# Turning the memory's normalized tokens into channels: squares of 32 on VectorE with a trip through DRAM, in place of identity matmuls

## The chip, the core and the metric

The kernel runs on one core of one Trainium2 chip. A core has TensorE (PE in the profile; its weight loads are listed apart as PEld), VectorE (DVE), ScalarE (ACT), GpSimd (POOL) and SyncE (SP), which here only issues DMAs. Each engine works off its own instructions in order and waits on semaphores for the others. The metric is the device time of one execution in microseconds (us), smaller being better. A change is judged by the medians of several runs before and after.

## What is computed

One layer of a streaming encoder on 512 tokens of 1024 channels. Four mixers run in parallel on the normalized input; their outputs are gated, merged and projected. Then comes cross-attention into 256 memory tokens, then a gated MLP. All inputs are float32. The change touches the way in which the memory tokens reach the cross-attention:

```python
def _rms_norm(x, g):
    y = xf * lax.rsqrt(jnp.mean(xf * xf, axis=-1, keepdims=True) + EPS)
    return (y * g.astype(jnp.float32)).astype(x.dtype)
...
x = x + _rms_norm(mixed, norm_mix_post[l])
hx = _rms_norm(x, norm_x_pre[l])
m = _rms_norm(mem, norm_mem[l])              # mem: (1, 256, 1024)
xq = (hx @ w_xq[l]).reshape(B, S, X_HEADS, X_HEAD_DIM)
xk, xv = jnp.split(m @ w_xkv[l], 2, axis=-1)
```

The product `m @ w_xkv` sums over the 1024 channels. TensorE sums over partitions, so the normalized tokens, which stand with tokens on partitions, must be turned so that channels stand on partitions.

## The kernel before

**Precision.** Every float32 operand of a product is held as two tiles, a rounded high part and the rest. `split` (L152) makes them: ScalarE copies the value into the high tile (L155), VectorE subtracts it from the value and leaves the low tile (L156). A product is three matmuls (`mm3`: high with high, high with low, low with high), all through `matmul` at L232, so L232 carries nearly all of TensorE's work. Weights come in pieces of 512 KB: `load_raw` issues the DMA on SP (L176) into one of two buffers named `wr`; `split_weights` makes `wh` (ScalarE, L190) and `wl` (VectorE, L191), four buffers each. The memory tokens' pair of tiles is `mth` and `mtl`, each 128 partitions x 8 groups of channels x 256 tokens.

**The order of the work.** `run_blocks` (L203) takes jobs one after the other. It traces the load and the split of a job's weights three jobs ahead, then the job's matmuls. Beside the jobs runs a planner, `Background` (L47). It holds generators such as `mem_task`; each `yield cost, wait` says what the step just traced costs and how long, on a clock that adds up the expected time of the matmuls (0.215 us for one over 512 columns), the next step is to be left alone. After each job, and in the middle of a job whose weights have eight groups of channels, `tick` lets due tasks take steps, as far as a credit of 0.7 us for each us of clock allows. `drain` runs a named task to its end. The traced order is not the order in the queues: a scheduler goes through the trace with a timeline of its own, and lays out the instructions of each engine and each DMA queue by when it expects them to be ready. So the queues of SP and ScalarE can stand in another order than the text.

**The stage of the change.** The last of the four mixers' gates is `gate_blocks(1, "f", ...)`: four times two gate jobs (24 matmuls into one PSUM bank, a tanh on ScalarE at L1043) and one branch job (24 matmuls into two banks, VectorE's multiply and add at L1055 and L1056). Banks come from `bank` (L97): here alternately from the names `mm` and `av`, with two banks each; transposes use the name `tr`. `open_last_branch` (L1130) opens the pool `xm`, issues the load of the memory norm's gain on POOL and adds `mem_task` to the planner. When the twelve jobs are traced, `all_jobs` drains `mem`, opens the merge (`open_mix_out`, which takes the tags `s0`, `s1` and `s2` again for two rows of gains and for `m1`), runs its jobs, and only then the first readers of `mth` and `mtl`, `kx_jobs` (L1180).

**The task.** `mem_task` (L1169) works on two blocks of 128 tokens. For each, POOL issues the load of the tokens into `m_t` (tag `s1`, one buffer, L1172), `normed` (L274) squares and sums on ScalarE (L277), makes the factor on POOL (L268, L271) and multiplies on VectorE (L281) into `y_t` (tag `s2`, one buffer, named `mn`). After a wait of 8 `to_channels` (L286) makes eight transposes of 128x128 on TensorE, as matmuls by the identity (L236), four in each of two banks, and splits each bank into `mth` and `mtl`.

**A trip through DRAM that the kernel already makes.** The convolution's output is turned twice, in `conv_norm_task` (L670). VectorE's `transpose` turns every square of 32x32 in place (L676). DMAs on SP write the squares to DRAM at their transposed places (L680), and read them back as rows (L683).

Of the kernel before, what the change touches and what calls it, by code (L numbers as in the profile page):

```python
# [17 lines left out]
F32 = mybir.dt.float32  # L18
# [7 lines left out]
P = 128  # L26
# [3 lines left out]
NK = D // P  # L30
# [53 lines left out]
def hybrid_layer(ctx: ExitStack, tc: tile.TileContext, a: dict, out: bass.AP):  # L84
    nc = tc.nc
    V, A, G, PE, SP = nc.vector, nc.scalar, nc.gpsimd, nc.tensor, nc.sync
# [4 lines left out]
    dram = ctx.enter_context(tc.tile_pool(name="dr", bufs=1, space=DRAM))  # L91
# [5 lines left out]
    def bank(tag=None):  # L97
        if tag is None:
            turn_of.n += 1
            tag = "av" if turn_of.shared and turn_of.n % 2 else "mm"  # L100
        return psum.tile([P, 512], F32, tag=tag, name=f"ps_{tag}", bufs=2)
# [24 lines left out]
    def space(pool, name, n):  # L126

        if n:
            pool.tile([P, n // 4], F32, name=name)

    for i in range(8):
        n = ("wh", "wl")[i % 2]
# [3 lines left out]
        elif i < 6:  # L136
            n = ("fz_raw", "fz", "fe", "fu", "fd")[i - 1]
# [14 lines left out]
    def split(ps, hi, lo, scale=None):  # L152

        if scale is None:
            A.copy(hi, ps)  # L155
            V.tensor_tensor(lo, ps, hi.bitcast(F32), ALU.subtract)  # L156
        else:
            A.activation(hi, ps, AF.Copy if isinstance(scale, float) else AF.Identity, scale=scale)
            V.scalar_tensor_tensor(lo, ps, scale, hi.bitcast(F32), ALU.mult, ALU.subtract)
# [75 lines left out]
    def transpose(ps, x, n=P):  # L235
        PE.transpose(ps, x, ident[:n, :n])  # L236
        bg.clock += 0.107
# [26 lines left out]
    def rstd_of(pool, parts, n=1):  # L264

        m = pool.tile([P, n], F32, tag="st_m", name="st_m", bufs=4)
        r = pool.tile([P, n], F32, tag="st_r", name="st_r", bufs=4)
        G.tensor_tensor(m, parts[0], eps[:, :n], ALU.add)  # L268
        for part in parts[1:]:
            G.tensor_tensor(m, m, part, ALU.add)  # L270
        G.tensor_tensor(r, m, nhalf[:, :n], ALU.pow)  # L271
        return r

    def normed(pool, x_t, gain, y_t, ends=None):  # L274

        ms = pool.tile([P, 1], F32, tag="st_s", name="st_s", bufs=4)
        A.activation(y_t, x_t, AF.Square, scale=1.0 / math.sqrt(D), accum_out=ms)  # L277
        r = rstd_of(pool, [ms])
        n = D // len(gain)
        for i, g in enumerate(gain):  # L280
            end = V.scalar_tensor_tensor(y_t[:, i * n:(i + 1) * n], x_t[:, i * n:(i + 1) * n], r, g, ALU.mult, ALU.mult)  # L281
        if ends is not None:
            ends.append(end.ins)
        return y_t

    def to_channels(y_t, act, t):  # L286

        sl = slice(t * P, (t + 1) * P)
        for half in range(2):
            ps = bank("tr")  # L290
            ks = slice(half * 4, half * 4 + 4)
            for k in range(4):
                transpose(ps[:, k * P:(k + 1) * P], y_t[:, (half * 4 + k) * P:(half * 4 + k + 1) * P])
            split(ps.rearrange("p (k c) -> p k c", k=4), act[0][:, ks, sl], act[1][:, ks, sl])
# [18 lines left out]
    def e4(dtype=F32):  # L313
        return m1p.tile([P, 2, S], dtype, tag="e", name="e", bufs=3)
# [55 lines left out]
    for i, plan in enumerate(plans):  # L370
        r_t = m1p.tile([P, P], F32, tag="fbias" if i == 2 else "ck", name=f"rows{i}", bufs=2)
        n = 0
# [19 lines left out]
    for t in range(2):  # L392
        y_t = m1p.tile([P, D], F32, tag="ptl", name="nt", bufs=2)
# [29 lines left out]
    def turn(t, half):  # L423
        ps = turned[t, half] = bank("av" if half else "tr")
        for k in range(4):
            keep(PE.transpose(ps[:, k * P:(k + 1) * P], y01[t][:, (half * 4 + k) * P:(half * 4 + k + 1) * P], ident))
# [54 lines left out]
    for i in range(2):  # L481
        for p in range(3):
            first_half(i, p, w_g[i], glu[2:])
            if p == 2 - 2 * i:
                with tc.issue_after(casts[-1].ins):
                    y_t = normed(m1p, xs[:, 2 + i], gain, m1p.tile([P, D], F32, tag="ptl", name="nt", bufs=2))
                to_channels(y_t, ht, 2 + i)

    def pc(name, j=0, n=1):
        i, base = where[name]  # L490
        return par[i][:, base + j:base + j + n]
# [89 lines left out]
    def y8(dtype=F32R):  # L581
        return m2p.tile([P, 4, S], dtype, tag="y8", name="y8", bufs=2)
# [73 lines left out]
    def conv_task(j):  # L656
# [5 lines left out]
        for k in range(n - 1):  # L662
# [4 lines left out]
                conv_ends.append(ins.ins)  # L667
            yield 0.66, 0.0

    def conv_norm_task():  # L670
        xn = m1p.tile([P, 5, S], F32, tag="qk", name="xn", bufs=2)
        tok, chan = (dram.tile([S, S], F32, name=n) for n in ("conv_tok", "conv_chan"))

        def turn(rows, squares, src):
            for i in range(4):
                V.transpose(squares[:, i], src[:, i])  # L676
                yield 0.65, 0.0
            form = rows.rearrange("(b r) (j a c) -> a r j b c", r=32, a=4, c=32)
            for a in range(4):
                SP.dma_start(form[a], squares[a * 32:a * 32 + 32].rearrange("r j (b c) -> r j b c", c=32))  # L680
            yield 0.0, 4.0
            for i in range(4):
                SP.dma_start(xn[:, i], rows[i * P:(i + 1) * P, :])  # L683
            yield 0.0, 5.0

        yield 0.0, 2.0
        while len(conv_ends) < 4:
            yield 0.0, 0.5
        yield from turn(tok, conv_u, conv_y)
        for t in range(NT):  # L690
            st = m1p.tile([P, 6], F32, tag="bn6", name="bn6", bufs=2)
            mv = m1p.tile([P, 2], F32, tag="bn2", name="bn2", bufs=2)
            V.bn_stats(st, xn[:, t])
            V.bn_aggr(mv, st)
            r = rstd_of(m1p, [mv[:, 1:2]])
            V.tensor_scalar(xn[:, t], xn[:, t], mv[:, 0:1], r, ALU.subtract, ALU.mult)
            yield 1.5, 0.0
        yield from turn(chan, conv_y, xn)
        while "d" in y:
            yield 0.0, 2.0  # L700
        yield 0.0, 2.0
        y["c"] = (y8(), y8())
        for j in range(4):
            e = e4()
            A.activation(e[:, 0], xn[:, j], AF.Identity, bias=pc("ln_b", j), scale=pc("ln_g", j))
            A.activation(e[:, 1], xn[:, j], AF.Tanh, bias=half["ln_b"][:, j:j + 1], scale=half["ln_g"][:, j:j + 1])
            V.scalar_tensor_tensor(e[:, 0], e[:, 1], 1.0, e[:, 0], ALU.add, ALU.mult)
            split(e[:, 0], y["c"][0][:, j], y["c"][1][:, j], 0.5)
            yield 1.4, 1.0
# [355 lines left out]
    ns = SimpleNamespace()  # L1065
# [8 lines left out]
    def mixer_jobs():  # L1074
        yield from c_jobs()
        yield then(lambda: bg.add(lam_task(), "lam"))
        yield from d_jobs()
        yield then(lambda: bg.add(conv_norm_task(), "conv"))
        wide = m1p.tile([P, NT, D], F32, tag="v", name="wide")
        free = iter([wide[:, i] for i in (0, 1, 2, 3) * 2])  # L1080
# [46 lines left out]
    def stage(tag, name):  # L1127
        return ns.xm.tile([P, D], F32, tag=tag, name=name)

    def open_last_branch():  # L1130
        close(m1)
        close(m2b)
        ns.xm_, ns.xm = new_pool("xm", True)
        ns.mt = (ns.xm.tile([P, NK, MEM], F32R, tag="mth", name="mth"),
                 ns.xm.tile([P, NK, MEM], F32R, tag="mtl", name="mtl"))
        ns.kx = (ns.xm.tile([P, 4, MEM], F32R, name="kxh"), ns.xm.tile([P, 4, MEM], F32R, name="kxl"))
        ns.gain = stage("s0", "g_mem")
        G.dma_start(ns.gain, a["norm_mem"][0].partition_broadcast(P))
        bg.add(mem_task(), "mem")
        ns.mix_, ns.mixp = new_pool("mix", True)  # L1140
        ns.mix, ns.mix_parts, ns.wide = {}, {}, None
        qa = [mix_tile("qa0", 4)]
        hl = [[mix_tile(f"m{i}{q}", 4, F32R) for i in range(2)] for q in range(NK // 2)]
        qa.append(mix_tile("qa1", 4))
        ns.mix_a, ns.mix_b, ns.mix_hl = qa, mix_tile("qb", 12), hl
# [23 lines left out]
    def mem_task():  # L1169
        for t in range(2):  # L1170
            m_t = stage("s1", "m_t")
            G.dma_start(m_t, mem_d[t * P:(t + 1) * P, :])  # L1172
            y_t = normed(ns.xm, m_t, [ns.gain], stage("s2", "mn"))
            if t == 0:
                space(ns.xm, "gap8", 96)
            yield 1.3, 8.0
            to_channels(y_t, ns.mt, t)
            yield 1.2, 0.0

    def kx_jobs():  # L1180
        for h in range(4):
# [573 lines left out]
```

## Time and profile before

| | |
|---|---|
| median of 3 runs | 1061.96 us (1061.37 to 1063.41) |
| the profiled execution | 1061.46 us, of it span of the trace 1059.7 us |
| mean granted clock of TensorE | 0.998 |
| TensorE busy | 1048.7 us |
| VectorE busy | 800.8 us |
| ScalarE busy | 497.9 us |
| moved by DMA | 156.78 MB, mean 148 GB/s |

The span runs from the first to the last instruction of the trace. "Busy" is the time in which an engine had an instruction under way; on TensorE neighbouring matmuls overlap, so that the time from one start to the next is shorter than the duration shown. In lists of instructions a line shows start, duration, engine, line of the program, operation, the tile written and the tiles read, and in brackets the idle time before it with what ended it.

### The profile page before, as it was taken

The numbers are of one execution on the slowest core, as the hardware profiler recorded it, in microseconds if no ns is written. First come the engines' busy times: TensorE is split into PE (matmuls) and PEld (weight loads), VectorE is DVE, ScalarE is ACT, GpSimd is POOL, SyncE is SP. The second block draws the span as 40 slices with busy tenths as digits, with TensorE's granted clock in tenths as the row PEclk, the third lists the DMA queues.
The fourth block names the chain that finished last, engine by engine and source line by source line (L and its number), as shares of the span: only waits on it lengthen the run. The fifth ranks groups of instructions, "written<-read, shape, count | busy, mean of one in ns | idle before, by whom it ended". The sixth has DMA issues, their size and how long they took to land.

```text
span 1059.7 us, 14546 instructions
## 1 busy us (share of the span) xinstructions
PE 1048.7 (99%) x5343; PEld 891.8 (84%) x5343; DVE 800.8 (76%) x1270; ACT 497.9 (47%) x819; POOL 150.8 (14%) x249
## 2 busy tenths in 40 slices
PE   9999999999999999999999999999999999999997
PEld 8888888878888988888888899999888888888886
DVE  6999997577666358766575888886778788777796
ACT  5322222277465255655443665654333333445672
POOL 4001000100001015322100031031111211111011
PEclk9999999999999999999999999999999999999999
DMA  8854335732222243322344734226566776725662
GB/s 269 300 153 104 104 97 128 198 113 80 80 80 68 59 135 100 97 84 80 120 140 154 268 133 120 80 81 199 179 229 211 235 230 209 236 80 179 210 216 80
DMA packets 179773, 156.78 MB, mean 148 GB/s; under 512 B 22207, under 2 KB 151852, under 8 KB 179701
## 3 DMA queue, kind: packets, MB, share of 16 engines
q1 hardware_dynamic: 170659, 124.10, 38.9%
q10 hardware_dynamic: 6482, 23.21, 5.8%
q0 software_dynamic: 2560, 8.54, 2.8%
q8 instruction: 42, 0.69, 0.3%
q14 instruction: 30, 0.25, 0.1%
HBM read 135.89 MB, written 19.94 MB: 147 GB/s over the span
## 4 chain that ended last, share of the span: by engine, by line
PE 95%; DMA 1%; DVE 1%; ACT 1%; issue 0%; POOL 0%; SPq 0%; POOLq 0%; DVEq 0%; ACTq 0%
PE ps_mm L232 51%; PE ps_av L232 29%; PE ps_sc L232 7%; PE ps_tr L232 4%; PE ps_tr L236 3%; DMA xn<-conv_tok 1%; PE ps_mm L442 1%; PE ps_av L442 1%; DMA conv_chan<-y 0%; PE ps_mm L384 0%; SPq L680 0%; PE ps_sc L389 0%; DMA xn<-conv_chan 0%; DVE wl L191 0%; POOL st_r L271 0%
## 5 line engine op out<-in xcount | busy, mean ns | idle before, releaser
L190 ACT CAST wh<-wr 128x1024 fp32r<-128x1024 f32 (+1 forms) x142 | 148.6, 1049 | 273.5 <-PE ps_mm L232 185.6
L191 DVE TENSOR_TENSOR wl<-wr,wh 128x1024 fp32r<-128x1024 f32 (+1 forms) x142 | 178.1, 1256 | 80.9 <-ACT wh L190 80.3
L232 PE MATMUL ps_mm<-hth,wh 128*128 128x512 f32 (+1 forms) x616 | 231.4, 382 | 2.4 <-DVE qk L777 1.9
L232 PE MATMUL ps_mm<-htl,wh 128*128 128x512 f32 (+1 forms) x616 | 230.1, 380 | 0.0
L232 PE MATMUL ps_mm<-hth,wl 128*128 128x512 f32 (+1 forms) x616 | 229.9, 380 | 0.0
L232 PEld LDWEIGHTS ps_mm<-hth,wh 128*128 128x128 f32 x616 | 114.1, 188 | 24.5 <-issue 2.3
L232 PEld LDWEIGHTS ps_mm<-hth,wl 128*128 128x128 f32 x616 | 114.0, 188 | 21.3
L232 PEld LDWEIGHTS ps_mm<-htl,wh 128*128 128x128 f32 x616 | 114.1, 188 | 20.3
L232 PE MATMUL ps_av<-htl,wh 128*128 128x512 f32 (+1 forms) x328 | 122.5, 373 | 0.0
L232 PE MATMUL ps_av<-hth,wh 128*128 128x512 f32 (+1 forms) x328 | 122.4, 373 | 0.0
L232 PE MATMUL ps_av<-hth,wl 128*128 128x512 f32 (+1 forms) x328 | 122.4, 373 | 0.0
L664 DVE SCALAR_TENSOR_TENSOR y<-y,par,y 128x482 f32<-128x482 f32 (+29 forms) x120 | 82.9, 727 | 0.2
L232 PEld LDWEIGHTS ps_av<-hth,wh 128*128 128x128 f32 x328 | 61.6, 188 | 10.9
L232 PEld LDWEIGHTS ps_av<-hth,wl 128*128 128x128 f32 x328 | 61.6, 188 | 10.9
L232 PEld LDWEIGHTS ps_av<-htl,wh 128*128 128x128 f32 x328 | 61.6, 188 | 10.8
L1548 DVE TENSOR_TENSOR wl<-dw,wh 128x1024 fp32r<-128x1024 f32 x32 | 40.2, 1260 | 13.2 <-ACT wh L1547 13.0
L1547 ACT CAST wh<-dw 128x1024 fp32r<-128x1024 f32 x32 | 33.4, 1051 | 23.3 <-PE ps_tr L232 8.5
L1002 POOL TENSOR_SCALAR fbias<-ck,cq 128x128 f32<-128x128 f32 (+3 forms) x32 | 27.5, 865 | 68.9 <-DVE st L1008 63.7
L1496 ACT ACTIVATE th<-c 128x512 f32<-128x512 f32 x22 | 13.9, 632 | 48.3 <-DVE c L594 48.2
L155 ACT CAST pth<-ps_tr 128x512 fp32r<-128x512 f32 (+3 forms) x56 | 23.4, 448 | 22.0 <-PE ps_tr L236 21.9
L594 DVE SCALAR_TENSOR_TENSOR c<-ps_mm,par,c 128x510 f32<-128x510 f32 (+1 forms) x44 | 32.7, 744 | 0.7
L156 DVE TENSOR_TENSOR ptl<-ps_tr,pth 128x512 fp32r<-128x512 f32 (+3 forms) x56 | 27.9, 513 | 6.1 <-ACT pth L155 5.9
(469 smaller groups left out, 2102.9 us busy)
## 6 DMA issues: line engine op xcount, KB each, us to landing
wr<-in_w_up SPq DMA_DIRECT2D x44, 512.0 KB
wr<-in_w_in SPq DMA_DIRECT2D x38, 512.0 KB
wr<-in_w_gate SPq DMA_DIRECT2D x32, 512.0 KB
wp<-in_w_down ACTq DMA_DIRECT2D x22, 512.0 KB
sums<-wp ACTq DMA_DIRECT2D x22, 512.0 KB
dw<-sums SPq DMA_DIRECT2D x44, 256.0 KB
wr<-in_w_branch SPq DMA_DIRECT2D x16, 512.0 KB
wide<-in_w_out SPq DMA_DIRECT2D x12, 512.0 KB
```

What stands on the lines that cost most here:

```text
L155: A.copy(hi, ps)
L156: V.tensor_tensor(lo, ps, hi.bitcast(F32), ALU.subtract)
L190: order(A.copy(hi, raw[:, :n]))
L191: low.tensor_tensor(lo, raw[:, :n], hi.bitcast(F32), ALU.subtract)
L232: PE.matmul(ps, lhs, rhs, start=start, stop=stop)
L236: PE.transpose(ps, x, ident[:n, :n])
L442: keep(PE.matmul(banks[c][:, :S // 2], w[p == 1][:, k, c * P:(c + 1) * P], ht[p == 2][:, i * 4 + k, :S // 2], start=(i, p, k) == (0, 0, 0) ...
L594: ins = V.scalar_tensor_tensor(dst[:, s:], src[:, :S - s], w(k), dst[:, s:], ALU.mult, ALU.add)
L664: ins = V.scalar_tensor_tensor(dst[:, s:], src[:, :S - s], pc("conv_dw", k * 4 + j), dst[:, s:], ALU.mult, ALU.add)
L1002: G.tensor_scalar(bias[:, :w], ck[j][:, :w], -1.0, cq[:, qt, head:head + 1], ALU.mult, ALU.add)
L1547: A.copy(hi, x)
L1548: V.tensor_tensor(lo, x, hi.bitcast(F32), ALU.subtract)
```

## The change

`to_channels` is no longer used for the memory. Two helpers come in. `squares` is one VectorE instruction that transposes each 32x32 square of a tile of 128x1024, and writes the squares in another order, so that for each of four blocks of 32 columns the eight groups of channels stand side by side. `turn` writes that tile (`m_t`, whose tokens are no longer needed) to DRAM with one DMA on SP, then reads it back into `y_t` with four DMAs on SP, one for each block of 32 partitions. Each piece that such a load moves in one run is 256 values, 1 KB. Then channels stand on partitions, and `split` makes the two halves of `mth` and `mtl` from `y_t` in SBUF rather than from PSUM. The planner's waits for one block become 3, 0.5, 4, 5, 1 and 1 in place of 8 and 0. `m_t` and `y_t` still have one buffer each, so the load of the second block's tokens has to wait for the store of the first, and the second block's norm for the splits of the first.

```diff
+    def squares(dst, src, n):
+
+        V.transpose(dst.rearrange("p (b n c) -> p n b c", b=4, c=32), src.rearrange("p (n b c) -> p n b c", b=4, c=32))
+
+    def turn(dst, src, n, between, name):
+
+        t = dram.tile([P, n * P], F32, name=name)
+        squares(between, src, n)
+        yield 0.1 + 0.14 * n, 0.5
+        SP.dma_start(t, between)
+        yield 0.0, 4.0
+        form = t.rearrange("(i r) (b x) -> b r i x", r=32, b=4)
+        for b in range(4):
+            SP.dma_start(dst[b * 32:b * 32 + 32].rearrange("r (i x) -> r i x", i=4), form[b])
+        yield 0.0, 5.0
...
             y_t = normed(ns.xm, m_t, [ns.gain], stage("s2", "mn"))
             if t == 0:
                 space(ns.xm, "gap8", 96)
-            yield 1.3, 8.0
-            to_channels(y_t, ns.mt, t)
-            yield 1.2, 0.0
+            yield 1.3, 3.0
+            yield from turn(y_t, y_t, NK, m_t, f"mem_chan{t}")
+            by_chan = y_t.rearrange("p (b k c) -> p k b c", b=4, k=NK)
+            for i in range(2):
+                ks = slice(i * 4, i * 4 + 4)
+                split(by_chan[:, ks], *(x[:, ks, t * P:(t + 1) * P].rearrange("p k (b c) -> p k b c", b=4) for x in ns.mt))
+                yield 0.7, 1.0
```

## The prediction

> **What bounds the kernel now.** I read the page first: the busy shares and the chain that ended last.
>
> ```profile
> PE 1048.7 (99%) x5343; PEld 891.8 (84%) x5343; DVE 800.8 (76%) x1270; ACT 497.9 (47%) x819; POOL 150.8 (14%) x249
> ...
> PE 95%; DMA 1%; DVE 1%; ACT 1%; issue 0%; POOL 0%; SPq 0%; POOLq 0%; DVEq 0%; ACTq 0%
> ```
>
> TensorE is busy 1048.7 of 1059.7 us, so what it issues sets the time, and its 11 us of idle time are the only reserve. Where they lie is in the busy time by stages (columns: stage, its length, then PE, PEld, DVE, ACT, POOL with counts, clock, DMA share, GB/s).
>
> ```profile
> 0.00:20.00 20.00, 18.43 (x113) 15.61 (x114) 13.75 (x22) 11.11 (x20) 12.41 (x26) 1.00 0.79 261
> 220.00:240.00 20.00, 18.13 (x86) 14.88 (x85) 14.23 (x34) 14.12 (x28) 1.04 (x2) 1.00 0.34 99
> 500.00:620.00 120.00, 120.00 (x568) 100.43 (x568) 82.93 (x117) 57.41 (x85) 10.29 (x18) 1.00 0.51 164
> 1040.00:1060.00 20.00, 12.71 (x68) 10.83 (x66) 13.22 (x21) 4.37 (x14) 5.20 (x12) 0.87 0.28 105
> ```
>
> The start holds 1.57 us of it, the stretch at 220 us 1.87, the tail 7.0. The edited stage (500 to 620 us, PE 120.00 of 120.00, granted clock 1.00) has none: a TensorE instruction removed there is gained whole, and a wait put there is lost whole. VectorE works 82.93 of those 120 us and has room.
>
> **The change part by part.** *Removed: 16 transposes on TensorE.* The chain of waits over that stretch, then the starts of the jobs in TensorE's timeline (start, duration):
>
> ```profile
> 541.96 0.87 PE ps_tr L236 x8
> 553.09 0.87 PE ps_tr L236 x8
> ```
>
> ```profile
> 539.98 0.62 PE L232 MATMUL ps_mm<-y,wh 128*128 128x512 f32 x2
> ...
> 546.35 0.39 PE L232 MATMUL ps_mm<-hth,wh 128*128 128x512 f32 x1
> ...
> 551.79 0.39 PE L232 MATMUL ps_av<-hth,wh 128*128 128x512 f32 x1
> ...
> 558.12 0.61 PE L232 MATMUL ps_mm<-y,wh 128*128 128x512 f32 x2
> ...
> 563.56 0.39 PE L232 MATMUL ps_mm<-hth,wh 128*128 128x512 f32 x1
> ...
> 569.00 0.39 PE L232 MATMUL ps_av<-hth,wh 128*128 128x512 f32 x1
> ```
>
> Each job is 24 matmuls. A job without transposes takes 563.56 - 558.12 = 5.44 us. The two that hold eight each take 546.35 - 539.98 = 6.37 and 558.12 - 551.79 = 6.33. So they cost 0.93 + 0.89 = **1.82 us** (the chain alone says 2 x 0.87; the rest is the matmul behind each group). I take 1.82, the difference that the stream itself shows.
>
> What an instruction occupies is not what it costs:
>
> ```profile
> L236 PE MATMUL ps_tr<-ident,mn x16: 270/272/273, 541.8 to 553.7; 128*128 128x128 f32 x16
> L277 ACT ACTIVATE mn<-m_t x2: 1056/1059/1062, 527.5 to 545.8; 128x1024 f32<-128x1024 f32 x2
> L281 DVE SCALAR_TENSOR_TENSOR mn<-m_t,st_r,g_mem x2: 1276/1277/1278, 536.2 to 548.2; 128x1024 f32<-128x1024 f32 x2
> ```
>
> A transpose is recorded with 272 ns, but eight advance the stream by 0.87, 109 ns each, since they overlap. The Trainium skill, page "VectorE: DVE Perf Modes", section "The three transpose paths", gives 390 ns for a 128x128 bf16 transpose on TensorE and 311 ns on VectorE, and "Rules for kernel authors" there sends 128x128 transposes to TensorE. By that figure the removal would be worth 16 x 0.39 = 6.24 us, an estimate from the page, and the end 1055.2; the trace does not agree, with 109 ns in this stream.
>
> *Added on VectorE: two transposes in squares, 128x1024 each.*
>
> ```profile
> L676 DVE STREAM_TRANSPOSE y<-y x4: 697/702/712, 103.1 to 176.6; 128x512 f32<-128x512 f32 x4
> ```
>
> At 0.70 for half the width each costs at most 1.40 us, 2.8 together; at least one of the 0.70 rows. I take 1.40. They lie beside TensorE on an engine with 37 free us in this stage: nothing on the path. With that cover gone, 2.8 us.
>
> *Moved: the splits read SBUF, not PSUM.* Count and size stay.
>
> ```profile
> L232 PE MATMUL ps_av<-mth,wh x16: 281/281/281, 618.0 to 628.9; 128*128 128x256 f32 x16
> L155 ACT CAST mth<-ps_tr x4: 577/583/599, 542.5 to 554.8; 128x512 fp32r<-128x512 f32 x4
> L156 DVE TENSOR_TENSOR mtl<-ps_tr,mth x4: 681/684/691, 543.1 to 556.2; 128x512 fp32r<-128x512 f32 x4
> ```
>
> Two casts and a subtraction behind them take 0.58 + 0.58 + 0.69 = 1.85 us per block of 128 tokens. The first matmul that reads the result starts at 618.0, so the memory now has 61 us of slack behind its last subtraction (556.2 + 0.69).
>
> *Added on SP's queue: ten DMAs*, a store of 512 KB and four loads of 128 KB for each block. The nearest rows are the convolution's own turns through DRAM, four DMAs each way; in the chain of waits a DMA stands from its issue to the wait that it ends:
>
> ```profile
> 185.35 5.85 DMA xn<-conv_tok
> ...
> 203.44 4.95 DMA conv_chan<-y
> ```
>
> ```profile
> 208.52 1.77 SPq L683 DMA_DIRECT2D xn<-conv_chan  x4
> ...
> 538.64 0.37 SPq L176 DMA_DIRECT2D wr<-in_w_branch  x1
> ```
>
> Both ways I take 4.95 to 5.85 us to land, and 0.44 us per issue (1.77 / 4). The chain of block 0 follows: the multiply ends at 536.2 + 1.28 = 537.5, the squares at 538.9, the store lands at 543.9 to 544.7, the last of four loads is issued 1.3 us later and lands at 550.2 to 551.9, the splits end at 552.0 to 553.8. Block 1 then has its tile free, needs 3.7 us to its multiply's end (548.2 + 1.28 - 545.8), 1.4 for the squares, and the same round trip: its loads land at 568.3 to 571.9, its splits end at 570.2 to 573.7. Against 618.0 that leaves 44 us. Also by the planner's own dues it fits: seven steps a block with waits of 3, 0.5, 4, 5, 1 and 1, taken at ticks 2.6 or 5.2 of its microseconds apart, end at 51.6 of the 61.9 that the twelve jobs before the drain last.
>
> *What is queued behind the new waits.* On SP the store waits for the squares and the loads for the store. Behind them stand the weight loads:
>
> ```profile
> 544.39 1.05 ACT L190 CAST wh<-wr 128x1024 fp32r<-128x1024 f32 x1 [1.33 <-DMA wr<-in_w_branch]
> ...
> 554.29 1.06 ACT L155 CAST mth<-ps_tr 128x512 fp32r<-128x512 f32 x2
> ...
> 559.09 0.68 ACT L1043 ACTIVATE ge<-ps_av,s_b_gate 128x512 f32<-128x512 f32 x1
> ...
> 569.97 0.68 ACT L1043 ACTIVATE ge<-ps_mm,s_b_gate 128x512 f32<-128x512 f32 x1
> ...
> 597.87 1.06 ACT L1314 COPY m<-ps_sc 128x512 f32<-128x512 f32 x2
> ```
>
> ```profile
> 545.47 1.23 DVE L191 TENSOR_TENSOR wl<-wr,wh 128x1024 fp32r<-128x1024 f32 x1 [0.98 <-ACT wh L190]
> ```
>
> The branch weights issued at 538.64 are the ones most exposed: they land at 544.39, are split by 546.7 and used at 558.12, 557.2 after the change, so 10.5 us of slack. Behind the store's issue alone they come 0.4 us later; behind store and loads together they are issued at 544.7 + 1.8 = 546.5, 7.9 us late. Neither reaches TensorE. Cost taken: nothing, with 10.5 - 7.9 = 2.6 us of slack left in the worse case. On POOL the second block's memory load now waits for the store:
>
> ```profile
> 537.78 0.59 POOL L1172 DMA_DIRECT2D m_t<-in_mem  x1 [8.24 <-DVE mn L281]
> ```
>
> It goes from 537.78 to about 544.3; behind it on POOL stands its own norm. The tile of the normalized tokens is next written at 597.87 (m), 24 us after the last split. These cost nothing.
>
> *Sum* against the profiled execution's own 1061.46 us (span 1059.7 and 1.76 around it): 1061.46 - 1.82 = 1059.64. Its runs have a median 0.50 above that execution, so among runs I expect 1061.96 - 1.82 = **1060.1**.
>
> **The rivals.** *A, slower: ScalarE stands in its queue before block 1's loads.* Both casts of a block need all four loads. If they are placed ahead of the tanh now at 559.09, that tanh cannot free its bank until they are through. The bank is the one that the gate job at 569.00 takes next (two banks of that name, the other taken in between by the branch), and after the change that job is due at 569.00 - 1.82 = 567.18. With the loads landing at x, the tanh ends at x + 1.06 + 0.69, and TensorE waits x + 1.75 - 567.18. For x from 568.3 to 571.9 this is 2.9 to 6.5 us, a net loss of 1.1 to 4.7; the middle, x = 570.1, gives +2.85, **1064.8** among runs. It eats the gain from x = 567.25, and costs over 0.2% from 569.4. For it speaks that engines here did stand waiting for such loads:
>
> ```profile
>   DMA xn<-conv_chan: 2.0, 1
>   DMA xn<-conv_tok: 1.1, 1
> ```
>
> Against it: those waits were 1 to 2 us, so the order allowed for most of the trip; ten microseconds of chain put the casts nearer the tanh at 569.97, whose bank is wanted only at 574.4.
>
> *B, no gain: the weights come late after all.* If the branch weights come 12.3 us later than now (10.5 of slack and 1.8 of stall), the gain is gone: 1061.96. The 7.9 worked out above would have to grow by half, for instance because 512 KB more share the DMA engines there. That the edit leaves TensorE's stream as it was is not possible, since no identity matmul is left in the block.
>
> *C, a larger gain:* if the stream really loses the whole 272 ns of each transpose, 16 x 0.272 = 4.35 us go, 1057.6 among runs. The job starts above speak against it. The page's 390 ns would be a stronger form of this.
>
> **How the numbers follow.** The forecast has 0.60, A 0.22, B 0.13, C 0.05. About 0.2%, 2.1 us, is what a measurement of this kernel can tell from no change; that line lies at 1059.84, just under the forecast. Its own range is 1058.8 to 1061.2 (half a microsecond of scatter between medians, and an order of instructions that is laid out anew behind the edit), so its 0.60 splits 0.32 faster and 0.28 same. Faster: 0.32 + 0.05 = 0.37; same: 0.28 + 0.13 = 0.41; slower: 0.22. The range 1058.6 to 1064.5 leaves out C and the upper half of A.
>
> **What would show it.** Right: jobs of 5.44 us all through 540 to 575, TensorE still 120 of 120 us there; two squares transposes of about 1.4 us; stores landing within 6 us; the first reader of the memory tile near 616. Wrong: any wait of TensorE between 540 and 620 (on the tanh's bank it is A, on a weight tile B), jobs that had taken more than 6.4, or a stall much later from an order laid out anew, which I price only in the scatter.

## The result, and the profile after

| | before | after |
|---|---|---|
| median (range) | 1062.24 us (1061.37 to 1063.41, 7 runs) | 1065.29 us (1062.71 to 1067.99, 7 runs) |
| ratio, 95% interval | | 1.0029 [1.0017, 1.0040] |
| profiled execution | 1061.46 us | 1067.99 us |
| TensorE busy | 1048.7 us | 1050.6 us |

The seven runs of before stand in place of the three that were known ahead of the prediction (1061.96). The change costs 3.05 us, about 0.3%. First the page of the changed kernel: busy times, and shares of the chain that ended last.

```profile
PE 1050.6 (99%) x5327; PEld 892.0 (84%) x5327; DVE 801.6 (75%) x1272; ACT 498.0 (47%) x819; POOL 149.7 (14%) x249
...
PE 88%; DMA 5%; DVE 2%; ACT 2%; issue 1%; SPq 1%; POOL 1%; POOLq 0%; DVEq 0%; ACTq 0%
```

TensorE has 16 instructions fewer, as it should, and is still busy longer; DMA's share of the chain went from 1% to 5%. The page says that a chain now runs through a transfer, not yet where.

**A common ruler.** The profiled execution of after reached the edited stage 4.0 us later than that of before, with the same instructions ahead of it. So positions can't be compared as they stand. About 3.4 of it is TensorE's own: idle time of 0.75 us at 29.89, 1.25 in place of 0.19 near 217, and a slow clock behind a pause at 225 (1.6), which the last section takes up. I measure from the issue of the memory gain's load to the first matmul that reads the memory tile. The rows of the tiles (lowest, median and highest duration in ns, first to last start), before first:

```profile
L1138 POOL DMA_DIRECT2D g_mem<-in_norm_mem x1: 577/577/577, 504.9 to 504.9; - x1
```

```profile
L1154 POOL DMA_DIRECT2D g_mem<-in_norm_mem x1: 577/577/577, 508.9 to 508.9; - x1
...
L232 PE MATMUL ps_av<-mth,wh x16: 281/281/281, 624.6 to 635.6; 128*128 128x256 f32 x16
```

Before, the stretch was 618.0 - 504.9 = 113.1 us; after, 624.6 - 508.9 = 115.7. The loss in this stretch is 2.6 us, nearly all of the difference of the medians. Below, a time of after "on the old clock" is its time less 4.0.

**The gain is there.** TensorE's timeline of after (start, duration), at the starts of the jobs:

```profile
549.39 0.39 PE L232 MATMUL ps_mm<-hth,wh 128*128 128x512 f32 x1
...
554.83 0.39 PE L232 MATMUL ps_av<-hth,wh 128*128 128x512 f32 x1
...
560.27 0.62 PE L232 MATMUL ps_mm<-y,wh 128*128 128x512 f32 x2
```

Both distances are 5.44 us; the two jobs of 6.37 and 6.33 are gone. The 1.82 us were gained.

**The loss is later.** Busy time by stages of after, in the columns explained above; then TensorE's waits (in total, times, longest):

```profile
500.00:580.00 80.00, 80.00 (x377) 66.80 (x376) 49.32 (x80) 30.89 (x52) 9.38 (x17) 1.00 0.49 138
...
585.00:590.00 5.00, 5.00 (x24) 4.11 (x22) 2.53 (x5) 0.00 (x0) 0.00 (x0) 1.00 1.01 355
590.00:595.00 5.00, 2.65 (x9) 1.70 (x8) 2.41 (x4) 1.88 (x2) 0.00 (x0) 0.92 1.03 331
595.00:600.00 5.00, 5.00 (x18) 3.96 (x18) 4.76 (x5) 5.00 (x7) 0.00 (x0) 0.74 0.93 310
```

```profile
PE ps_mm L232 <- ACT wh L155: 1.6, 1, 1.6
PE ps_mm L232 <- DVE wl L156: 0.8, 1, 0.8
```

Up to 580 TensorE never stops. Between 590 and 595 it does, twice, on weight tiles of the merge. In the 5 us behind it, it counts as fully busy and yet holds 18 matmuls where the window from 585 to 590 holds 24, at a granted clock of 0.74. The stream itself gives the price:

```profile
589.97 0.39 PE L232 MATMUL ps_tr<-wh,mix 128*128 128x512 f32 x1
591.94 0.50 PE L232 MATMUL ps_mm<-wh,mix 128*128 128x512 f32 x1 [1.59 <-ACT wh L155]
593.21 0.50 PE L232 MATMUL ps_mm<-wl,mix 128*128 128x512 f32 x1 [0.76 <-DVE wl L156]
...
594.25 0.63 PE L232 MATMUL ps_mm<-wh,mix 128*128 128x512 f32 x1
...
597.66 0.40 PE L232 MATMUL ps_sc<-wl,mix 128*128 128x512 f32 x1
```

From 589.97 to 597.66 TensorE advances by 14 matmuls in 7.69 us. At the usual 5.44 / 24 = 0.227 us a matmul that is 3.17 us of work, so 4.5 us are lost. The two stops account for 2.8 of it (1.97 - 0.23 and 1.27 - 0.23), and most of the rest falls between 594.25 and 597.66: eight matmuls in 3.41 us instead of 1.81, the slow clock. Lost 4.5 less gained 1.8 is 2.7, against the 2.6 of the ruler.

**Why the merge's weights are late.** The chain of waits of after, cut to its steps from the memory's DMAs to the stop:

```profile
545.25 5.24 DMA mem_chan<-m_t
...
551.90 6.74 DMA mn<-mem_chan
...
573.95 6.02 DMA wr<-in_w_out
...
581.69 1.24 DVE wl L156
582.95 0.38 SPq L176
583.37 0.59 SPq L561
584.00 6.74 DMA wide<-out_sums
590.85 1.05 ACT wh L155
```

Read it from the end. TensorE waits for `wh`, cast at 590.85 from `wide`. The `wide` loads stand on SP behind the load of `w_xq` (L176, 582.95), which waits until the buffer `wr` is free, that is until VectorE has made `wl` out of it (581.69 + 1.24 = 582.93). VectorE waits for ScalarE's cast of merge job 1's weights, at 580.61. ScalarE's and SP's timelines of after say why that is late:

```profile
558.74 1.14 ACT L155 CAST mth<-mn 128x512 fp32r<-128x512 f32 x2 [8.28 <-DMA mn<-mem_chan]
...
579.57 1.14 ACT L155 CAST mth<-mn 128x512 fp32r<-128x512 f32 x2 [5.33 <-DMA mn<-mem_chan]
580.61 1.05 ACT L155 CAST wh<-wr 128x1024 fp32r<-128x1024 f32 x1
```

```profile
566.96 0.33 SPq L679 DMA_DIRECT2D mem_chan<-m_t  x1
...
571.98 1.88 SPq L683 DMA_DIRECT2D mn<-mem_chan  x4
...
582.95 0.38 SPq L176 DMA_DIRECT2D wr<-in_w_xq  x1
583.37 1.11 SPq L561 DMA_DIRECT2D wide<-out_sums  x2
```

The scheduler put block 1's casts (579.57) ahead of merge job 1's weight cast (580.61) in ScalarE's queue. ScalarE stood idle 5.33 us for block 1's loads, with that cast behind it.

One step of the chain needs care. It follows ScalarE back to the landing of `wr<-in_w_out` (573.95 + 6.02 = 579.97). Those are the weights of merge job 2, which stand on SP behind block 1's loads. But block 1's casts had begun at 579.57, released by block 1's own loads, and job 1's cast doesn't need job 2's weights: in the last run below it started 1.05 us after their issue (573.45 - 572.40).

Before, three timelines (ScalarE, VectorE, SP) show the same cast, buffer and loads:

```profile
569.02 1.05 ACT L155 CAST wh<-wr 128x1024 fp32r<-128x1024 f32 x1 [0.69 <-PE ps_mm L232]
```

```profile
570.10 1.23 DVE L156 TENSOR_TENSOR wl<-wr,wh 128x1024 fp32r<-128x1024 f32 x1 [0.51 <-ACT wh L155]
```

```profile
571.36 0.38 SPq L176 DMA_DIRECT2D wr<-in_w_xq  x1
574.63 0.80 SPq L561 DMA_DIRECT2D wide<-out_sums  x2
```

The link holds there too: 570.10 + 1.23 = 571.33, and the `w_xq` load goes at 571.36. On the old clock the cast is 580.61 - 4.0 = 576.6, 7.6 us late; `w_xq` is 7.6 late as well, and `wide`, which had 2.9 us of room behind it (574.63 - 571.36 - 0.38), is 4.7 late.

**The edit's own pieces**, from VectorE's timeline of after:

```profile
540.18 1.28 DVE L281 SCALAR_TENSOR_TENSOR mn<-m_t,st_r,g_mem 128x1024 f32<-128x1024 f32 x1
...
543.98 1.24 DVE L672 STREAM_TRANSPOSE m_t<-mn 128x1024 f32<-128x1024 f32 x1
```

The squares take 1.24 us, but start 2.5 us after the multiply's end (541.46), behind other work that the scheduler put first. The store takes 5.24 us to land, the loads 6.74 after the last issue.

### The profile page after: what moved, and what is told of

It is laid out like the page before. It is cut to its first block, busy times and chain, and to the rows that moved or that the text cites. A ratio compares the mean times of both kernels' runs of the same rounds, so it can differ in the third digit from the quotient of the medians.

```text
span 1066.2 us, 14537 instructions
## 1 busy us (share of the span) xinstructions
PE 1050.6 (99%) x5327; PEld 892.0 (84%) x5327; DVE 801.6 (75%) x1272; ACT 498.0 (47%) x819; POOL 149.7 (14%) x249
## 4 chain that ended last, share of the span: by engine, by line
PE 88%; DMA 5%; DVE 2%; ACT 2%; issue 1%; SPq 1%; POOL 1%; POOLq 0%; DVEq 0%; ACTq 0%
PE ps_mm L232 48%; PE ps_av L232 26%; PE ps_sc L232 7%; PE ps_tr L232 3%; PE ps_tr L236 3%; DMA mem_chan<-m_t 1%; DMA mn<-mem_chan 1%; DMA wide<-out_sums 1%; DMA wr<-in_w_out 1%; DMA wide<-in_w_out 1%; ACT wh L190 1%; DMA xn<-conv_tok 1%; SPq L696 0%; DMA conv_chan<-y 0%; PE ps_mm L384 0%
```

## The experiments

The question is which link makes the loss. Three readings stand against each other, by the letters that the expectations use. **Q**: SP's order alone, the merge's loads queued behind block 1's store and loads. **E**: ScalarE standing alone, wherever its casts wait for a trip. **C** (not the prediction's rival C): the whole chain, casts ahead of job 1's weight cast, hence the buffer late, hence `w_xq` and `wide` late. All twelve kernels were timed in rounds beside the kernel before, whose median was 1062.49, 1062.50 and 1062.68 us in the three batches (35 runs each). The ratio with its interval is the measurement's own, not the quotient of the two medians. The stretch is the ruler from above (113.1 before, 115.7 after), taken in each kernel's own profile.

| kernel | stretch | median (range), us | ratio [95%] |
|---|---|---|---|
| no trip | 111.2 | 1060.35 (1059.10 to 1064.08) | 0.9985 [0.9975, 0.9995] |
| trip not waited for | 112.8 | 1062.20 (1060.48 to 1066.64) | 1.0004 [0.9991, 1.0017] |
| trip on POOL | 111.2 | 1061.24 (1059.35 to 1062.53) | 0.9983 [0.9974, 0.9992] |
| trip on POOL, splits later | 111.2 | 1062.59 (1059.82 to 1065.20) | 0.9999 [0.9988, 1.0010] |
| splits later, on SP | 115.1 | 1063.81 (1062.32 to 1066.01) | 1.0015 [1.0007, 1.0024] |
| block 1 alone on SP | 111.2 | 1061.11 (1059.29 to 1062.96) | 0.9989 [0.9980, 0.9998] |
| block 0 alone on SP | 111.2 | 1059.84 (1059.03 to 1063.58) | 0.9984 [0.9974, 0.9993] |
| stores on SP, loads on POOL | 111.2 | 1061.99 (1059.69 to 1063.91) | 0.9992 [0.9979, 1.0006] |
| the change once more | 116.2 | 1066.05 (1063.45 to 1069.77) | 1.0031 [1.0018, 1.0045] |
| block 1 behind on SP | 111.2 | 1061.83 (1059.66 to 1065.73) | 0.9992 [0.9981, 1.0003] |
| block 1 ahead on SP | 111.2 | 1061.26 (1058.40 to 1063.20) | 0.9982 [0.9971, 0.9992] |
| casts behind, SP unchanged | 111.2 | 1061.08 (1059.53 to 1061.98) | 0.9982 [0.9973, 0.9991] |

A stretch of 111.2 is 113.1 less 1.9: the removed transposes and nothing lost. The runs fall into those that have it and those that stall. Each stretch comes from one profile, while the ratio rests on 11 or 12 runs.

**No trip.** Only the squares are left, and the splits read them.

```diff
-            yield from turn(y_t, y_t, NK, m_t, f"mem_chan{t}")
-            by_chan = y_t.rearrange("p (b k c) -> p k b c", b=4, k=NK)
+            squares(m_t, y_t, NK)
+            yield 1.2, 0.5
+            by_chan = m_t.rearrange("p (b k c) -> p k b c", b=4, k=NK)
```

> The two squares stay, the store and the loads are left out, and the splits read the squares' tile on the chip: the rows of mth and mtl are then not those of whole channels. Theory Q (the weight loads stand behind the trip's DMAs on SP's queue) and theory E (ScalarE and VectorE stand in their queues before the trip's loads) both expect what is left when the trip costs nothing: 1.8 us under the kernel before, about 1060.4, and no wait of TensorE between 500 and 620 us. If a third cause is at work (the squares themselves, or the order laid out anew), it stays above 1062.

Measured 111.2 and 0.9985, with no wait of TensorE from 500 to 640. Removing the transposes is worth what the prediction said, VectorE's squares cost nothing in the stretch, and the whole loss hangs on the trip.

**Trip not waited for.** The ten DMAs stay on SP, but the splits read `m_t`.

```diff
-            by_chan = y_t.rearrange("p (b k c) -> p k b c", b=4, k=NK)
+            by_chan = m_t.rearrange("p (b k c) -> p k b c", b=4, k=NK)
```

> The trip stays on SP as in the changed kernel, but the splits read the squares' tile on the chip, so nobody but the next block's norm waits for the loads (mth and mtl then do not hold whole channels). Theory E: no engine stands before the loads, about 1060.4 to 1061. Theory Q: the weight loads still stand behind the trip on SP, and the stall remains, 1064 or more.

Measured 112.8, a loss of 1.6 beside the run without the trip, and waits of 0.8 and 0.2 us on `wl` of the merge. Its ScalarE and SP timelines:

```profile
578.60 1.05 ACT L155 CAST wh<-wr 128x1024 fp32r<-128x1024 f32 x1 [4.59 <-DMA wr<-out_sums]
```

```profile
580.93 0.38 SPq L176 DMA_DIRECT2D wr<-in_w_xq  x1
```

Here the same weight cast is late for another reason: a load of its own weights went behind block 1's loads on SP. From the cast on it is the same chain, `w_xq` at 580.93 and `wide` behind it. So Q can do harm by itself when the order falls so, through the same last links, but it gives less than the whole.

**Trip on POOL.** Store and loads go to GpSimd's queue.

```diff
-        SP.dma_start(t, between)
+        G.dma_start(t, between)
...
-            SP.dma_start(dst[b * 32:b * 32 + 32].rearrange("r (i x) -> r i x", i=4), form[b])
+            G.dma_start(dst[b * 32:b * 32 + 32].rearrange("r (i x) -> r i x", i=4), form[b])
```

> The store and the four loads are issued on POOL in place of SP. Theory Q: the weight loads go past them, the stall near 590 us is gone, about 1060.4 to 1061. Theory E: the splits still wait for the loads on ScalarE and VectorE, the merge's weight casts are still late, 1064 or more.

Measured 111.2 and 0.9983. ScalarE still stood 4.19 us before block 1's casts, yet TensorE didn't wait, which speaks against E. But the scheduler, freed of SP, also put the weight cast ahead of block 1's casts, so two links were cut at once.

**Splits later, on POOL and on SP.** The splits are traced to come behind the merge's weight casts, with the trip on POOL in one kernel and on SP in the other.

```diff
-            yield from turn(y_t, y_t, NK, m_t, f"mem_chan{t}")
+            yield from turn(y_t, y_t, NK, m_t, f"mem_chan{t}", (26.0, 5.0)[t])
...
+                with tc.issue_after(latest["hi"]), tc.issue_after(latest["lo"]):
```

> The trip on POOL, and the splits of both blocks held behind the weight casts traced up to then on ScalarE and VectorE, so that neither SP nor an engine stands before the trip. Both theories: the whole gain of 1.8 us, about 1060.4. If it stays above 1062, something else costs, such as the 2 MB more on the DMA engines.

> Both trips on SP, and the splits held behind the weight casts traced up to then, so that ScalarE and VectorE do not stand before the loads; block 1's trip moves back behind the merge's first weights on SP with that. Theory E alone: a stretch near 111.2, about 1060.5. Theory Q: SP now stands before block 1's store and loads among the merge's wide loads, and the stall stays or grows, a stretch of 113 or more.

On POOL: the stretch shows no stall, while the median stayed above 1062 and the interval of the ratio holds 1; by time it is inconclusive, and a cost outside the stretch isn't excluded. On SP it was a miss: 115.1 and 1.0015. Holding the splits back moved block 1's whole trip later, in among the `wide` loads on SP, and its casts came in front of a later weight cast. ScalarE's timeline there:

```profile
591.32 1.14 ACT L155 CAST mth<-mn 128x512 fp32r<-128x512 f32 x2 [6.87 <-DMA mn<-mem_chan]
```

Here too weight casts of the merge stood behind a trip (593.11), and TensorE stopped for 1.5 and 0.3 us on `wh` and `wl`. Moving the trip later changed the victim. It changed SP's order as well, so this run doesn't tell Q from the casts. Nor does every weight cast behind a trip stall TensorE: with the trip on POOL, job 2's cast stood behind block 1's casts (576.50) and nothing came of it.

**One block on SP, the other on POOL.**

```diff
-            yield from turn(y_t, y_t, NK, m_t, f"mem_chan{t}")
+            yield from turn(y_t, y_t, NK, m_t, f"mem_chan{t}", (G, SP)[t])
```

> Block 0's trip on POOL, block 1's on SP. The stretch from the issue of the memory gain's load to the first matmul that reads mth is 113.1 us in the kernel before, 115.7 after the change, 111.2 without the trip. Theory Q2 (what costs is block 1's four loads on SP ahead of the merge's weight loads, the last of the chain before the stall): a stretch of 113 to 116, a stall on the merge's weights, 1063 or more. If the delay has to build up over both blocks, a stretch near 111.5 and about 1060.5.

and with `(SP, G)[t]`:

> Block 0's trip on SP, block 1's on POOL; ScalarE's order for block 0 is that of the changed kernel, so it stands before block 0's loads as there. Theory Q2: the weights behind block 0's trip have over 10 us of slack, a stretch of 111.2 to 111.6, no stall, about 1060.5. If block 0's waits (on SP or on ScalarE) carry over into the merge, 113 or more.

Both measured 111.2. With block 0 on SP its casts stood as in after:

```profile
554.00 1.14 ACT L155 CAST mth<-mn 128x512 fp32r<-128x512 f32 x2 [7.73 <-DMA mn<-mem_chan]
```

7.73 us of standing cost nothing: block 0 is harmless, and E as a general rule falls. With block 1 on SP alone Q2 expected the loss, and it didn't come; the scheduler had put job 1's weight cast ahead of block 1's casts. So that run didn't tell a build-up over both blocks from the order.

**Stores on SP, loads on POOL.**

```diff
-            SP.dma_start(dst[b * 32:b * 32 + 32].rearrange("r (i x) -> r i x", i=4), form[b])
+            G.dma_start(dst[b * 32:b * 32 + 32].rearrange("r (i x) -> r i x", i=4), form[b])
```

> Both stores on SP, all loads on POOL. A store waits on SP only for the squares, a load for the store's landing, 5 us. If it is the wait for the landing that holds SP up: a stretch near 111.2, about 1060.5. If the wait for the squares is enough: 113 or more, and a stall on the merge's weights.

Measured 111.2; ScalarE stood 6.87 us for block 1's loads and nothing came of it. The stores on SP are harmless in this order; job 1's cast (568.66) had come ahead of block 1's (577.15) here too. The ratio's interval just holds 1, so the gain is shown by the stretch only.

**The change once more, and three orders set by hand.** The last batch sets the order by hand. First the changed kernel again:

> The changed kernel once more, beside the others: 1065, ratio 1.003, a stretch of 115.7 us from the issue of the memory gain's load to the first matmul that reads mth, and a stall of TensorE on the merge's weights near 590 us.

Measured 116.2 and 1.0031, with TensorE's waits 2.1 and 0.8 us: the loss repeats. Then block 1's loads behind merge job 2's weight loads on SP, and its splits behind the casts of jobs 1 and 2:

```diff
+        yield 0.0, (4.0, 60.0)[block]
...
+            with tc.issue_after(latest["sp"]) if block else ExitStack():
+                latest["turn"] = SP.dma_start(dst[b * 32:b * 32 + 32].rearrange("r (i x) -> r i x", i=4), form[b]).ins
...
+                with tc.issue_after(latest["hi"]) if t else ExitStack(), tc.issue_after(latest["lo"]) if t else ExitStack():
```

> Both trips on SP, block 0 as in the changed kernel; block 1's loads held behind the weight loads of the merge's job 2 on SP, its splits behind the weight casts of jobs 1 and 2 on ScalarE and VectorE. Theory C (a chain: block 1's casts stand before job 1's weight cast, so its wr buffer comes free late, so the w_xq load that waits for that buffer holds up the wide loads behind it on SP) expects a stretch of 111.2 to 111.6 and 1060.5. So does theory Q. If block 0's delay alone reaches the merge: 113 or more.

Measured 111.2, ratio 0.9992 with an interval that holds 1: no stall, with all DMAs on SP. C and Q both expected it; block 0's delay alone doesn't reach the merge. Then the opposite, block 0 on POOL and block 1 on SP, its loads and casts forced ahead of the merge's:

```diff
+                with tc.issue_after(latest["turn"]) if len(raws) == 2 else ExitStack():
...
+            with tc.issue_after(latest["mth"]) if n == 1 else ExitStack(), tc.issue_after(latest["mtl"]) if n == 1 else ExitStack():
+                cast = A.copy(hi, raws[n])
```

> Block 0 on POOL; block 1 on SP with its loads ahead of the weight loads of the merge's job 2, and its casts ahead of the weight casts of jobs 1 and 2; the w_xq load now comes behind the first wide loads on SP. Theory C: the link from the wr buffer to the wide loads is cut, a stretch of 111.2 to 111.8. Theory E (casts standing before block 1's loads are enough): 113 or more.

Measured 111.2, as C expects and E doesn't. Its ScalarE and SP timelines:

```profile
575.75 1.14 ACT L1203 CAST mth<-mn 128x512 fp32r<-128x512 f32 x2 [5.83 <-DMA mn<-mem_chan]
576.79 2.00 ACT L1311 CAST wh<-wr 128x1024 fp32r<-128x1024 f32 x2
```

```profile
574.66 0.80 SPq L563 DMA_DIRECT2D wide<-out_sums  x2
...
579.13 1.52 SPq L176 DMA_DIRECT2D wr<-in_w_xq  x2
```

ScalarE stood 5.83 us with the weight casts behind it, as in after, and SP's order was bad too. But in this order the `w_xq` load had fallen behind the first `wide` loads, so these didn't wait for the buffer. The last link was cut, and the stall is gone. Two things differ from after besides it. Block 0 is on POOL, harmless by the run above. And block 1's casts start 1.7 us earlier on the old clock (575.75 - 1.9 = 573.9, against 575.6; this kernel's ruler starts at 506.8, 1.9 behind before's). With `wide` still behind `w_xq` it would have gone near 579.13 + 0.38 = 579.5, on the old clock 3.0 late where after has 4.7. By that estimate about 1.1 of after's 2.8 us of stops would have stayed, and none did. Q and E together are not enough without the last link, but this run alone doesn't give it the whole loss.

**Casts behind, SP unchanged.** SP's order is left as in after; only block 1's splits are held behind the weight casts of merge jobs 1 and 2.

```diff
-        yield 0.0, 5.0
+        yield 0.0, (5.0, 60.0)[block]
...
+                with tc.issue_after(latest["hi"]) if t else ExitStack(), tc.issue_after(latest["lo"]) if t else ExitStack():
+                    latest["mth"] = A.copy(hi, by_chan[:, ks]).ins
+                    latest["mtl"] = V.tensor_tensor(lo, by_chan[:, ks], hi.bitcast(F32), ALU.subtract).ins
```

> SP's queue in the order of the changed kernel for both trips; only the splits of block 1 are held behind the weight casts of the merge's jobs 1 and 2 on ScalarE and VectorE. Theory C: the chain is cut at the cast, a stretch of 111.2 to 111.8, 1060.5 to 1061. Theory Q (SP's order alone): 113 or more, 1063 or more.

ScalarE's timeline, SP's, then the ruler's rows of this kernel:

```profile
573.45 1.05 ACT L1311 CAST wh<-wr 128x1024 fp32r<-128x1024 f32 x1 [0.50 <-DMA wr<-out_sums]
...
580.31 1.14 ACT L1203 CAST mth<-mn 128x512 fp32r<-128x512 f32 x2
```

```profile
570.56 1.74 SPq L687 DMA_DIRECT2D mn<-mem_chan  x4
572.40 0.38 SPq L563 DMA_DIRECT2D wr<-in_w_out  x1
575.78 0.38 SPq L176 DMA_DIRECT2D wr<-in_w_xq  x1
```

```profile
L1158 POOL DMA_DIRECT2D g_mem<-in_norm_mem x1: 577/577/577, 507.4 to 507.4; - x1
...
L234 PE MATMUL ps_av<-mth,wh x16: 281/281/281, 618.6 to 629.6; 128*128 128x256 f32 x16
```

618.6 - 507.4 = 111.2, ratio 0.9982 [0.9973, 0.9991]. Block 1's loads still stand ahead of the weight loads on SP, in the same order of loads as in after, but with the weight cast ahead of block 1's casts it comes at 573.45 and `w_xq` goes at 575.78. This kernel's ruler starts 2.5 behind before's (507.4 - 504.9), so on the old clock the cast comes at 571.0 and `w_xq` at 573.3, where after has 576.6 and 579.0, and the stall is gone. Of the 7.6 us by which after's cast was late, 5.7 were the order's; the other 1.9, still there, are its own weights' late landing, and cost nothing. This cuts the first link alone. C is shown at both of its ends, by this run and, with the estimate said there, by the one before it; Q's order is there in both and costs nothing in them.

Five versions of the whole change have an interval below 1, with ratios of 0.9982 to 0.9989: trip on POOL, block 1 alone on SP, block 0 alone on SP, block 1 ahead on SP, and casts behind. Among themselves their intervals overlap; the runs don't rank them. Trip on POOL is the simplest of them.

## Why the prediction was wrong

It said 1060.1 us, 1058.6 to 1064.5; the median was 1065.29, above the range. Point by point:

- **Removed transposes, 1.82 us: right.** Jobs of 5.44 us, and stretches 1.9 shorter wherever nothing stalls. The 1060.1 itself is about what the five good versions measure (1059.84 to 1061.26, beside a before of 1062.49 to 1062.68).
- **Squares at most 1.40 us, beside other work: right** (1.24). But the chain of block 0 started them straight behind the multiply; they came 2.5 us later.
- **Trip of 4.95 to 5.85 us each way: right for the store** (5.24), too small for block 0's loads (6.74 behind the last issue). Both errors make the casts later than the chain of block 1 had it: predicted landing 568.3 to 571.9, measured 579.57 - 4.0 = 575.6. Still far ahead of the first reader: the 44 us of slack were real, and beside the point.
- **"What is queued behind the new waits": the step that failed.** It followed the branch weights behind block 0's store and loads, found 7.9 us late against 10.5 of slack, and wrote "Neither reaches TensorE. Cost taken: nothing". For block 0 that was right; in after the load it followed even went ahead of block 0's store, on time (542.62 - 4.0 = 538.6). It stopped there: block 1's trip holds up another set of instructions, the merge's weights, and the path goes over two queues. Waiting casts on ScalarE keep a buffer full, the buffer holds a load on SP, and that load stands ahead of the loads that TensorE needs. Each queue was looked at alone, and the slack of one load stood for all. In place of nothing, the runs show 4.5 us lost at the merge.
- **Rival A, 0.22, 1064.8:** the right place (ScalarE stands before block 1's loads) and nearly the right time, with the wrong victim. It put the loss on the tanh's bank; TensorE's two waits are on weight tiles. By the prediction's own list of signs that was to be rival B, which had the cause in the branch weights. No case named the merge.
- **No price for the pause's aftermath.** A and B counted a pause at its length. Here 2.8 us of pauses cost 4.5. At its length alone the loss would have been 1.0 us net, about 1063, inside the range.
- **"An order of instructions that is laid out anew" was counted as half a microsecond of scatter.** The prediction's last sign of being wrong, a stall much later from such an order, is what came. The order was the mechanism: the casts' position is the scheduler's choice, and runs with the same DMAs differ by 4.5 us in the stretch with it (115.7 and 111.2).

## What to carry to other kernels

When an edit puts a transfer in front of an instruction on an in-order engine, list what stands behind that instruction, for every copy of the edit, and follow each item on: which buffer it frees, which load waits for that buffer, what stands behind that load in its queue. Slack at the edit's own reader says nothing about that chain. Where a scheduler orders the queues, pin the waiting instruction behind the ones that free buffers, or put the trip on a queue with nothing urgent in it.

## What was not expected of the hardware

A short pause of TensorE can cost more than its length. First the stages around a pause near 222 us that all kernels have, from before and from block 1 behind on SP; then the merge's stall in the changed kernel run again:

```profile
220.00:225.00 5.00, 3.13 (x15) 2.28 (x14) 4.76 (x8) 4.60 (x7) 1.04 (x2) 1.00 0.40 110
225.00:230.00 5.00, 5.00 (x26) 4.21 (x25) 2.25 (x8) 2.61 (x4) 0.00 (x0) 1.00 0.40 108
```

```profile
220.00:225.00 5.00, 3.17 (x12) 2.28 (x11) 4.80 (x7) 4.22 (x7) 1.04 (x2) 0.87 0.43 107
225.00:230.00 5.00, 5.00 (x21) 4.02 (x19) 0.84 (x2) 1.39 (x3) 0.00 (x0) 0.79 0.40 104
```

```profile
590.00:595.00 5.00, 4.24 (x11) 3.11 (x12) 4.93 (x7) 3.88 (x5) 0.00 (x0) 0.66 1.07 358
```

In before, 1.87 us of idle time left the clock at 1.00, and the next 5 us hold 26 matmuls. In the other kernel the same pause, 1.83 us with no idle time in the 5 us ahead of it, brought the clock to 0.87 and 0.79, and the next 5 us hold 21. All fourteen profiles have this pause, with 1.83 to 1.88 us. The clock fell behind it in six of them, after's among them, and stayed at 1.00 in eight. Behind the stall of the merge it was 0.74 in after and 0.66 in the second profile. At the lower clock matmuls start 0.43 us apart (eight in 3.41) instead of 0.227, and it lasted about 3.4 us, so each such fall costs about 1.6 us (3.41 - 1.81). The executions scatter by that too; the ruler leaves the pause near 222 us out.

The Trainium skill, page "TensorE: Matmul & The Clock Gate", section "HAM oscillation — how this bites in real kernels", gives the rule as no idle gap of TensorE over about 3.4 us. Here one gap of 1.83 us was enough in one profile, and one of 1.87 us was not in another, so the measurement asks for more caution than that rule. What decides stays open. It is not the length alone, and not whether a second pause lies close by: in trip not waited for, pauses of 1.97 and 0.31 us at 398 us, with two matmuls recorded between them, left the clock at 1.00.
